# Attention scores of the second block: two heads in TensorE's row halves instead of stacked parts

## The chip, the cores and the metric

The kernel runs on one core of one Trainium2 chip. The metric is the time of one execution in device microseconds (us), the median of three runs. TensorE does the matrix products into PSUM, VectorE (DVE), ScalarE (ACT) and GpSimd (POOL) do the rest, and SyncE (SP) issues most of the DMAs.

## The reference, cut to what matters

Three transformer-like blocks follow one another on 1024 tokens. The change is in the second one, in its attention: eight query heads of 64 dimensions share two key and value heads, four query heads each, and every query looks at 1024 tokens of the sequence and 256 tokens of a context (1280 keys, no mask).

```python
def block_attention(q, k, v):
    ...
    def attend(qblk):
        s = jnp.einsum('bqkgd,bskd->bkgqs', qblk, k, preferred_element_type=jnp.float32) * scale
        p = jax.nn.softmax(s, axis=-1).astype(v.dtype)
        return jnp.einsum('bkgqs,bskd->bqkgd', p, v)
...
    q = qk_heads(p[..., OFF_Q:OFF_K], N_Q_HEADS, q_gain, rope)
    k = qk_heads(p[..., OFF_K:OFF_V], N_KV_HEADS, k_gain, rope)
...
        att = block_attention(q, jnp.concatenate([k, k_ext], axis=1), jnp.concatenate([v, v_ext], axis=1))
```

## The kernel before, in words

Products that need more precision than one pass of the type F32R gives are made of parts: a number is split into a high part and a remainder (`C.split`: a copy on ACT, a subtraction on DVE), and the products high x high, low x high and high x low are summed in PSUM. Products of F32R operands show as one weight load and one matmul each. Products of plain F32 operands show as two of each, the transposes aside.

`attention2` first makes the keys and values, and then runs a loop over 16 units; a unit is one head with one half (512) of the tokens. `scores` (from line 1219) makes for each of the unit's four tiles of 128 tokens a row of 1280 scores, in three slices of 512, 512 and 256 keys. A head has 64 dimensions, so a query tile `aQ` holds the high part in one half of the 128 partitions and the low part in the other, and the keys' tiles `aKH` and `aKL` hold the same 64 rows twice. One matmul with `aKH` (L1230) and one with `aKL` (L1231) make a slice in one PSUM bank of the tag `t`, which has two banks. The slice is then copied into the tile `P` (L1232), by ACT, or by DVE for every other short slice. `softmax_sb` (L371 to L374) takes the maximum on DVE and the exponential on ACT.

`values` calls `pv_steps` (L340 to L363): the probabilities are transposed on TensorE (L344, tag `s`), split into `pth` and `ptl` (L143, L144), and multiplied with the values (L357, tag `a`, where the product with `ptl` is 64 columns wide). At the end the sums of the softmax are spread over 64 partitions by TensorE (L1240, F32), multiplied in, and written to DRAM (L1242).

Beside the units run jobs: products of 512 tokens with a tile of the input weights (L212, L213, L215, 24 matmuls for each bank of the tag `mm`), for the gates and for the next queries. `evq` takes the queries through a norm and a rotation and splits them (L1127, L1128). The order of all instructions on each engine is written at build time by a scheduler that may move an instruction past others on its engine where data and buffers allow; on the chip each engine takes its instructions in that order, and a wait holds up all that stands behind it.

Two places elsewhere use row halves of TensorE: L2444 in the third block's scan (64 rows, 128 columns, the two halves of the partitions in two banks) and L2229 in that block's preparation (64 rows, 512 columns, one call for each half). L1295 is a product of 64 rows that uses one half alone.

Of the kernel before, what the change touches and what calls it, by code (L numbers as in the profile page):

```python
# [10 lines left out]
F32 = mybir.dt.float32  # L11
F32R = mybir.dt.float32r
# [8 lines left out]
T = 1024  # L21
D = 1024
KD = 8
HALF = (slice(0, 512), slice(512, 1024))
# [1035 lines left out]
def qk_norm(C, pool, ps, gain, rope, perm, blk2, bufs=3):  # L1060

    nc = C.nc
    n = ps.shape[1]
    new = lambda: pool.tile([128, n], F32, name="tmp", tag="tmp")
    u = pool.tile([128, n], F32, name="qu", tag="qu", bufs=bufs)
    nc.scalar.copy(u, ps)
    rb = yield from head_norm(C, pool, u, n, blk2, 1.0 / 64, 1e-6)
    nc.vector.scalar_tensor_tensor(u, u, gain, rb, op0=OP.mult, op1=OP.mult)
    if rope is None:
        return u  # L1070
    yield
    p2 = C.bank(n)
    nc.tensor.matmul(p2, perm, u, start=True, stop=True)
    q = new()
    nc.gpsimd.tensor_mul(q, u, rope[:, 0])
    t = new()
    nc.vector.tensor_mul(t, p2, rope[:, 1])
    nc.gpsimd.tensor_add(q, q, t)
    return q


def attention2(C, hx, mod, mod_rest, dr, gates):


    nc = C.nc
    NS = 1280
    with C.pool("at") as p:
        KH = p.tile([128, 2, NS], F32R, name="aKH")
        KL = p.tile([128, 2, NS], F32R, name="aKL")
        V = p.tile([128, 10, 2, 128], F32R, name="aV")  # L1090
# [27 lines left out]
        Q, new_q, nq = {}, {}, 3  # L1118

        def evq(ft, half, ps):  # L1120
            u = yield from qk_norm(C, q, ps, C.vec("q_gain"), rope[:, :, HALF[half]], perm, blk2, nq)
            for e in range(2):
                r, r2 = slice(e * 64, e * 64 + 64), slice(64 - e * 64, 128 - e * 64)
                if half == 0:
                    new_q[e] = p.tile([128, T], F32R, name="aQ", tag="aQ", bufs=3)
                t = new_q[e]
                nc.scalar.copy(t[r, HALF[half]], u[r])  # L1127
                nc.vector.tensor_sub(t[r2, HALF[half]], u[r], t[r, HALF[half]].bitcast(F32))  # L1128
                if half == 1:
                    Q[2 * ft + e] = t  # L1130

        with C.pool("atc", bufs=4) as q:
            bd = cload(C, q, "k_bd", [128, 256], "bd", 1)
# [54 lines left out]
            r = C.rsqrt(C.colsum(acc, 256, 1.0 / D, 1e-6, "s"), 2)  # L1188
# [3 lines left out]
            for k in range(KD):  # L1192
                modulated(C, q, ct[:, k, :], 256, rb, mod[:, 6, k:k + 1], mod[:, 7, k:k + 1], hc, k)
            C.add("w2_in", [4, 5], hc, KD, 256, evc)
            C.add("w2_in", [0], hx, KD, T, evq)
            C.add("w2_in", range(6, 12), hx, KD, T, evh)
            C.add("w2_in", [12, 13], hx, KD, T, evf)
            C.run()

        with C.pool("atq", bufs=4) as q:  # L1200
            nq = 2

            jobs = gates(q)
            share = sum(t for _, _, t, _ in jobs) / 512 / 16
            count, credit = [], 0.0
            for u in range(16):
                take = []
                if u in (2, 6, 10):
                    take.append((u // 4 + 1, hx, T, evq))
                credit += share  # L1210
                while jobs and credit > 0.5:
                    take.append(jobs.pop(0))
                    credit -= take[-1][2] / 512
                count.append(sum(j[2] // 512 for j in take))
                for ft, rhs, t, ev in take:
                    C.add("w2_in", [ft], rhs, KD, t, ev)
            rest = mod_rest(q)

            def scores(h, half):
                while h not in Q:  # L1220
                    C.run(1)
                    if not C.jobs:
                        C.ahead()
                kv, P, R = h // 4, [], []
                for tb in range(4):
                    t0 = half * 512 + tb * 128
                    P.append(q.tile([128, NS], F32, name="P2", tag="P2", bufs=5))
                    for s in (slice(0, 512), slice(512, 1024), slice(1024, NS)):
                        b = C.bank(s.stop - s.start, "t")
                        nc.tensor.matmul(b, Q[h][:, t0:t0 + 128], KH[:, kv, s], start=True, stop=False)  # L1230
                        nc.tensor.matmul(b, Q[h][:, t0:t0 + 128], KL[:, kv, s], start=False, stop=True)  # L1231
                        (nc.vector.tensor_copy if s.start == 1024 and tb % 2 else nc.scalar.copy)(P[tb][:, s], b)  # L1232
                    R.append(C.softmax_sb(P[tb], 0.125))
                return h, half, P, R

            def values(h, half, P, R):
                def done(o):
                    b = C.bank(512)[0:64]
                    for tb in range(4):
                        nc.tensor.matmul(b[:, tb * 128:(tb + 1) * 128], R[tb].to_broadcast([128, 64]), C.ident, start=True, stop=True)  # L1240
                    nc.vector.tensor_mul(o, o, b)
                    nc.sync.dma_start(dr["att"][(h % 2) * 64:(h % 2) * 64 + 64, h // 2, HALF[half]], o)  # L1242

                C.pv(q, P, [V[:, j, h // 4, :] for j in range(10)], None, done, "s", 2)

            prev = None
            for u in range(17):
                cur = scores(u // 2, u % 2) if u < 16 else None
                if prev:
                    values(*prev)  # L1250
                prev = cur
                C.run(count[u] if u < 16 else None)
                if u >= REST:
                    for n in range(3):
                        next(rest, None)
            C.run()
            for _ in rest:
                pass
# [670 lines left out]
class Block2:  # L1929
# [79 lines left out]
    def run(self):  # L2009
# [963 lines left out]
```

## Time and profile before

| what | value |
|---|---|
| median of 3 runs | 3925.28 us (3924.64 to 3925.58) |
| profiled execution, its time | 3927.95 us |
| profiled execution, its span | 3926.2 us |
| granted TensorE clock, mean of the span | 0.975 |
| TensorE matmuls busy | 3667.1 us (93%) |
| VectorE busy | 2926.9 us (75%) |
| ScalarE busy | 2113.3 us (54%) |

Busy time of TensorE is to be read with care: a matmul's duration in the trace covers the way of its data through the array, and the next one starts before it ends. What a matmul costs in a stream is the distance from its start to the start of the next.

### The profile page before, as it was taken

The page shows a single profiled execution, that of the slowest core. Times are in us where ns is not written, and L with a number is a line of the kernel's source. Part 1 is how long each engine was busy: PE and PEld are TensorE (multiplying, and loading weights), DVE is VectorE, ACT ScalarE, POOL GpSimd, SP SyncE. Part 2 cuts the span into 40 slices and gives each one's busy share as a digit, 9 for nine tenths or more (in the row PEclk, how much of TensorE's full clock was granted, in tenths as well). Part 3 has the DMA queues.
Part 4 walks back from the last instruction along what each step waited for, and adds up shares of the span by engine and source line. Part 5 has one row for each costly group of instructions (what it writes and reads, how often), then busy time and mean ns, then how long its engine had stood idle before and what let it go on. Part 6 is the DMA issues. An engine that isn't in the chain of part 4 may idle for free. (4 is left out here: it accounts for less than half of the span.)

```text
span 3926.2 us, 53474 instructions
## 1 busy us (share of the span) xinstructions
PE 3667.1 (93%) x19084; PEld 2864.8 (73%) x19084; DVE 2926.9 (75%) x4681; ACT 2113.3 (54%) x3248; POOL 593.9 (15%) x439
## 2 busy tenths in 40 slices
PE   7998889999999988989599999999999899989998
PEld 5786677787777667876488777777777577767776
DVE  6758867555888775666899898888988645577765
ACT  4536644436777533223578777767767543334533
POOL 2111122000000233432111000000000111320011
PEclk9999999999999999999799999999999899999999
DMA  3431125432232247656799999999999323332462
GB/s 106 137 91 46 49 94 157 155 89 86 83 101 79 73 139 242 214 192 222 254 347 381 357 353 370 353 359 369 360 348 359 113 86 123 110 108 63 120 181 71
DMA packets 303844, 739.94 MB, mean 188 GB/s; under 512 B 62711, under 2 KB 103287, under 8 KB 302168
## 3 DMA queue, kind: packets, MB, share of 16 engines
q1 hardware_dynamic: 287640, 681.72, 49.9%
q0 software_dynamic: 13632, 46.40, 4.2%
q10 hardware_dynamic: 2304, 8.39, 0.5%
q8 instruction: 150, 2.46, 0.3%
q14 instruction: 118, 0.97, 0.1%
HBM read 640.42 MB, written 89.42 MB: 186 GB/s over the span
## 5 line engine op out<-in xcount | busy, mean ns | idle before, releaser
L1772 DVE TENSOR_TENSOR ewl<-er,ewh 128x1024 fp32r<-128x1024 f32 x543 | 634.9, 1222 | 65.6 <-ACT ewh L1771 62.9
L1771 ACT CAST ewh<-er 128x1024 fp32r<-128x1024 f32 x546 | 545.5, 1051 | 63.6 <-PE s L1826 25.7
L144 DVE TENSOR_TENSOR wlo<-wlo,whi 128x1024 fp32r<-128x1024 f32 (+2 forms) x155 | 187.0, 1207 | 234.0 <-PE mm L215 143.7
L212 PE MATMUL mm<-ygh,whi 128*128 128x512 f32 x736 | 299.2, 408 | 7.2 <-ACT whi L143 3.9
L213 PE MATMUL mm<-ygl,whi 128*128 128x512 f32 x736 | 297.0, 404 | 1.2 <-DVE ygl L144 1.2
L143 ACT CAST whi<-wlo 128x1024 fp32r<-128x1024 f32 (+2 forms) x155 | 152.4, 983 | 237.3 <-PE mm L213 165.5
L215 PE MATMUL mm<-ygh,wlo 128*128 128x512 f32 x736 | 196.2, 401 | 0.0
L212 PEld LDWEIGHTS mm<-ygh,whi 128*128 128x128 f32 x736 | 140.7, 192 | 44.9 <-ACT whi L143 7.0
L1826 PE MATMUL s<-ewl,xsh 128*128 128x512 f32 x512 | 162.4, 398 | 9.9 <-DVE ewl L1772 9.9
L212 PE MATMUL mm<-hnh,whi 128*128 128x512 f32 x416 | 166.5, 400 | 1.4 <-DVE QS L306 0.9
L213 PEld LDWEIGHTS mm<-ygl,whi 128*128 128x128 f32 x736 | 140.5, 191 | 36.2 <-issue 4.2
L1826 PE MATMUL mm<-ewl,xsh 128*128 128x512 f32 x512 | 161.0, 396 | 6.3 <-DVE ewl L1772 6.3
L215 PEld LDWEIGHTS mm<-ygh,wlo 128*128 128x128 f32 x736 | 139.3, 190 | 36.1 <-issue 3.9
L1826 PE MATMUL s<-ewh,xsh 128*128 128x512 f32 x512 | 160.6, 395 | 4.9 <-ACT xsh L143 4.9
L213 PE MATMUL mm<-hnl,whi 128*128 128x512 f32 x416 | 164.7, 396 | 0.0
L1826 PE MATMUL s<-ewh,xsl 128*128 128x512 f32 x512 | 162.1, 394 | 0.0
L1826 PE MATMUL mm<-ewh,xsh 128*128 128x512 f32 x512 | 159.2, 392 | 0.5
L1826 PE MATMUL mm<-ewh,xsl 128*128 128x512 f32 x512 | 158.1, 390 | 0.0
L1772 DVE TENSOR_TENSOR ewl<-wlo,ewh 128x1024 fp32r<-128x1024 f32 x126 | 148.8, 1219 | 9.9 <-ACT ewh L1771 9.3
L1771 ACT CAST ewh<-wlo 128x1024 fp32r<-128x1024 f32 x126 | 128.9, 1054 | 16.6 <-PE s L1826 9.1
L144 DVE TENSOR_TENSOR ptl<-s,pth 128x512 fp32r<-128x512 f32 x160 | 108.0, 686 | 24.4 <-ACT pth L143 17.1
L1855 POOL DMA_INDIRECT moed<-ys,topi x16 | 57.5, 3592 | 445.5 <-DVE ys L1854 445.5
(936 smaller groups left out, 9955.2 us busy)
## 6 DMA issues: line engine op xcount, KB each, us to landing
er<-w_up SPq DMA_DIRECT2D x183, 512.0 KB, 7.0
er<-w_down SPq DMA_DIRECT2D x182, 512.0 KB, 5.7
er<-w_gate SPq DMA_DIRECT2D x181, 512.0 KB, 6.9
wlo<-w_in SPq DMA_DIRECT2D x101, 512.0 KB, 3.7
wlo<-w_up SPq DMA_DIRECT2D x45, 512.0 KB, 7.1
wlo<-w_gate SPq DMA_DIRECT2D x43, 512.0 KB, 5.9
wlo<-w_out SPq DMA_DIRECT2D x40, 512.0 KB, 3.7
wlo<-w_down SPq DMA_DIRECT2D x38, 512.0 KB, 7.2
```

Source lines behind the costliest of these rows:

```text
L143: self.nc.scalar.copy(hi, src)
L144: (eng or self.nc.vector).tensor_sub(lo, src, hi.bitcast(F32))
L212: m(b, w.hi[:, k, :], rhs.hi[:, k - k0, s], start=(k == order[0]), stop=False)
L213: m(b, w.hi[:, k, :], rhs.lo[:, k - k0, s], start=False, stop=False)
L215: m(b, w.lo[:, k, :], rhs.hi[:, k - k0, s], start=False, stop=(k == order[-1]))
L1771: nc.scalar.copy(s.hi, raw)
L1772: (nc.gpsimd if i < 6 and i % 2 == 0 else nc.vector).tensor_sub(s.lo, raw, s.hi.bitcast(F32))
L1826: m(b[n], a[:, k, :], r[:, n * 512:(n + 1) * 512], start=(k == 0 and c == 0), stop=(k == KD - 1 and c == 2))
L1855: nc.gpsimd.indirect_dma_start(out=dr["moe"], out_offset=bass.IndirectOffsetOnAxis(ap=topi[:, e:e + 1], axis=0), in_=ys, in_offset=None, c ...
```

## The change

A unit becomes a pair of heads with a quarter (256) of the tokens, 16 units as before. The query tile of a pair holds the high part of both heads, one in each half of the partitions (`aQh`), and a second tile holds the low parts (`aQl`). For each tile of 128 tokens and each slice of keys, two banks of the tag `t` are taken, one for each head, and each gets three products of 64 rows. The two heads' calls alternate in the code. The splitting of the queries becomes one copy and one subtraction over 128 partitions in place of two over 64. The tiles `P` of scores have six buffers in place of five, and the result of a unit is written in two pieces.

```diff
         def evq(ft, half, ps):
             u = yield from qk_norm(C, q, ps, C.vec("q_gain"), rope[:, :, HALF[half]], perm, blk2, nq)
-            for e in range(2):
-                r, r2 = slice(e * 64, e * 64 + 64), slice(64 - e * 64, 128 - e * 64)
-                if half == 0:
-                    new_q[e] = p.tile([128, T], F32R, name="aQ", tag="aQ", bufs=3)
-                t = new_q[e]
-                nc.scalar.copy(t[r, HALF[half]], u[r])
-                nc.vector.tensor_sub(t[r2, HALF[half]], u[r], t[r, HALF[half]].bitcast(F32))
...
+            if half == 0:
+                new_q[0] = newsp(p, [128, T], "aQ", 2)
+            t = new_q[0][:, HALF[half]]
+            C.split(t.hi, t.lo, u)
...
-                kv, P, R = h // 4, [], []
-                for tb in range(4):
-                    t0 = half * 512 + tb * 128
-                    P.append(q.tile([128, NS], F32, name="P2", tag="P2", bufs=5))
+                kv, P, R = j // 2, [None] * 4, [None] * 4
+                rows = (slice(0, 64), slice(64, 128))
+                for tb in range(2):
+                    t = slice(part * 256 + tb * 128, part * 256 + tb * 128 + 128)
+                    two = [q.tile([128, NS], F32, name="P2", tag="P2", bufs=6) for _ in rows]
                     for s in (slice(0, 512), slice(512, 1024), slice(1024, NS)):
-                        b = C.bank(s.stop - s.start, "t")
-                        nc.tensor.matmul(b, Q[h][:, t0:t0 + 128], KH[:, kv, s], start=True, stop=False)
-                        nc.tensor.matmul(b, Q[h][:, t0:t0 + 128], KL[:, kv, s], start=False, stop=True)
-                        (nc.vector.tensor_copy if s.start == 1024 and tb % 2 else nc.scalar.copy)(P[tb][:, s], b)
-                    R.append(C.softmax_sb(P[tb], 0.125))
+                        b = [C.bank(s.stop - s.start, "t") for _ in rows]
+                        for n, (x, k) in enumerate(((Q[j].hi, KH), (Q[j].lo, KH), (Q[j].hi, KL))):
+                            for e, r in enumerate(rows):
+                                nc.tensor.matmul(b[e], x[r, t], k[r, kv, s], start=(n == 0), stop=(n == 2))
+                        for e in range(2):
+                            (nc.vector.tensor_copy if s.start == 1024 and e else nc.scalar.copy)(two[e][:, s], b[e])
...
-                    nc.sync.dma_start(dr["att"][(h % 2) * 64:(h % 2) * 64 + 64, h // 2, HALF[half]], o)
+                    for e in range(2):
+                        nc.sync.dma_start(dr["att"][e * 64:e * 64 + 64, j, part * 256:part * 256 + 256], o[:, e * 256:e * 256 + 256])
```

What the scheduler makes of it on TensorE is seen at two places. The first is where the first scores stand; a number behind `t` names a bank, so 7830 and 7831 are the two heads of one slice. Before:

```order
L212 MATMUL mm_7918<-ygh,whi 128x512
L1230 MATMUL t_7833<-aKH,aQ 128x512
L1231 MATMUL t_7833<-aKL,aQ 128x512
L213 MATMUL mm_7918<-ygl,whi 128x512
L1230 MATMUL t_7837<-aKH,aQ 128x512
L1231 MATMUL t_7837<-aKL,aQ 128x512
L212 MATMUL mm_7918<-ygh,whi 128x512
```

Of the change, at the same place (all score products now have line 1231):

```order
L212 MATMUL mm_7926<-ygh,whi 128x512
L1231 MATMUL t_7830<-aKH,aQh 128x512
L1231 MATMUL t_7830<-aKH,aQl 128x512
L1231 MATMUL t_7830<-aKL,aQh 128x512
L1231 MATMUL t_7831<-aKH,aQh 128x512
L1231 MATMUL t_7831<-aKH,aQl 128x512
L1231 MATMUL t_7831<-aKL,aQh 128x512
L213 MATMUL mm_7926<-ygl,whi 128x512
```

The three products of a head moved together, and the six of a slice stand between two matmuls of a job. The second place is the start of a later unit of TensorE's order. Before:

```order
L344 MATMUL s_8268<-ident,P_7992 128x128
L1230 MATMUL t_8192<-aKH,aQ 128x512
L1231 MATMUL t_8192<-aKL,aQ 128x512
L1230 MATMUL t_8196<-aKH,aQ 128x256
L1231 MATMUL t_8196<-aKL,aQ 128x256
L344 MATMUL s_8277<-ident,P_7992 128x128
```

Of the change:

```order
L1231 MATMUL t_8210<-aKH,aQh 128x512
L1231 MATMUL t_8210<-aKH,aQl 128x512
L1231 MATMUL t_8210<-aKL,aQh 128x512
L213 MATMUL mm_8457<-ygl,whi 128x512
L212 MATMUL mm_8457<-ygh,whi 128x512
L213 MATMUL mm_8457<-ygl,whi 128x512
L212 MATMUL mm_8457<-ygh,whi 128x512
L1231 MATMUL t_8211<-aKH,aQh 128x512
L1231 MATMUL t_8211<-aKH,aQl 128x512
L1231 MATMUL t_8211<-aKL,aQh 128x512
```

Here the two heads of a slice were moved apart, with four matmuls of a job between them. Over the whole stage the 576 score products of the change stand in 120 runs (products of line 1231 with nothing else between them): 43 runs hold both heads of slices of 512 keys (one of them two slices), 21 both heads of a slice of 256 keys, 6 one head of a long slice with one of a short slice, 34 one head of a long slice alone and 16 one head of a short slice alone. TensorE's order differs in names alone up to the stage's last jobs of the queries, and again from some 700 rows behind the last score on; in between it is shifted in places.

## Rows read from the trace of the kernel before

**Rows 1.** Span and mean granted TensorE clock of the core.

```profile
core 0: 3926.2 us, clock 0.975
```

**Rows 2.** Stretches: length, busy us of PE, PEld, DVE, ACT, POOL, PEclk, DMA.

```profile
908.00:1311.00 403.00, 397.47 (x2143) 305.15 (x2143) 326.13 (x667) 307.10 (x531) 17.33 (x12) 1.00 0.27 83
1311.00:1341.00 30.00, 30.00 (x120) 21.50 (x119) 17.63 (x35) 9.43 (x13) 0.00 (x0) 1.00 0.45 142
```

**Rows 3.** Timeline, PE: start us, us, engine, line, operation, tiles, shapes, count.

```profile
909.24 0.39 PE L1230 MATMUL t<-aKH,aQ 128*128 128x512 f32 x1
909.47 0.39 PE L1231 MATMUL t<-aKL,aQ 128*128 128x512 f32 x1
...
911.09 2.03 PE L215 MATMUL mm<-ygh,wlo 128*128 128x512 f32 x8
...
913.18 0.28 PE L1230 MATMUL t<-aKH,aQ 128*128 128x256 f32 x1
913.30 0.28 PE L1231 MATMUL t<-aKL,aQ 128*128 128x256 f32 x1
```

**Rows 4.** Who waited in the attention's units: total us, times, longest.

```profile
PEld t L1230 <- ACT P L1232: 17.3, 57, 1.2
```

**Rows 5.** Line L1230 (L1231 has as many): duration ns min/median/max, first and last start, forms.

```profile
L1230 PE MATMUL t<-aKH,aQ x192: 276/396/794, 908.4 to 1294.5; 128*128 128x512 f32 x128, 128*128 128x256 f32 x64
```

**Rows 6.** Timeline, PE, around a use of both row halves in the third block.

```profile
3604.89 0.28 PE L150 MATMUL s<-uvh,ckvl 128*128 128x128 f32 x1
3605.01 0.28 PE L151 MATMUL s<-uvl,ckvh 128*128 128x128 f32 x1
3605.21 1.16 PE L2444 MATMUL mm<-TB,Z 64*128 64x128 f32 x16
3606.30 0.33 PE L149 MATMUL s<-knh,qnh 128*128 128x128 f32 x1
3606.47 0.28 PE L150 MATMUL s<-knh,qnl 128*128 128x128 f32 x1
```

**Rows 7.** Timeline, PE, around another use of both halves, 512 columns.

```profile
3166.51 2.03 PE L215 MATMUL mm<-u0h,wlo 128*128 128x512 f32 x8
3168.47 1.13 PE L2229 MATMUL s<-xwa,wa 64*128 64x512 f32 x4
3169.53 0.50 PE L212 MATMUL mm<-u1h,whi 128*128 128x512 f32 x1
3169.87 0.40 PE L213 MATMUL mm<-u1l,whi 128*128 128x512 f32 x1
```

**Rows 8.** A stream that uses one row half alone: timeline, then the line's durations.

```profile
1345.08 4.13 PE L1295 MATMUL s<-w,hc 64*128 64x512 f32 x9
...
L1295 PE MATMUL s<-w,hc x32: 589/589/694, 1345.1 to 1366.9; 64*128 64x512 f32 x32
```

**Rows 9.** Timeline, PE: narrow products of F32R in the attention's units.

```profile
930.32 1.10 PE L215 MATMUL mm<-ygh,wlo 128*128 128x512 f32 x4
931.26 0.39 PE L357 MATMUL a<-ptl,aV 128*64 128x512 f32 x1
931.49 0.60 PE L344 MATMUL s<-ident,P 128*128 128x128 f32 x4
```

**Rows 10.** Line L1232, the copies of scores, and who waited for them.

```profile
L1232 ACT COPY P<-t x160: 366/587/608, 912.2 to 1294.4; 128x512 f32<-128x512 f32 x128, 128x256 f32<-128x256 f32 x32
...
  PEld t L1230: 20.2, 67
```

**Rows 11.** Lines L1127 and L1128, the split of the queries, and who waited.

```profile
L1127 ACT CAST aQ<-tmp x16: 614/619/625, 818.6 to 1217.9; 64x512 fp32r<-64x512 f32 x16
L1128 DVE TENSOR_TENSOR aQ<-tmp,aQ x16: 684/686/1643, 820.3 to 1218.8; 64x512 fp32r<-64x512 f32 x16
...
  PE t L1230: 0.8, 1
```

**Rows 12.** Line L1242, the DMA of a unit's result.

```profile
L1242 SPq DMA_DIRECT2D dAtt<-oh x16: 451/452/469, 946.3 to 1315.0; - x16
```

More of the change, by code (lines that the diff above doesn't have):

```diff
@@ L1121, in evq @@
             u = yield from qk_norm(C, q, ps, C.vec("q_gain"), rope[:, :, HALF[half]], perm, blk2, nq)
-            for e in range(2):
-                r, r2 = slice(e * 64, e * 64 + 64), slice(64 - e * 64, 128 - e * 64)
-                if half == 0:
-                    new_q[e] = p.tile([128, T], F32R, name="aQ", tag="aQ", bufs=3)
-                t = new_q[e]
-                nc.scalar.copy(t[r, HALF[half]], u[r])
-                nc.vector.tensor_sub(t[r2, HALF[half]], u[r], t[r, HALF[half]].bitcast(F32))
-                if half == 1:
-                    Q[2 * ft + e] = t
+            if half == 0:
+                new_q[0] = newsp(p, [128, T], "aQ", 2)
+            t = new_q[0][:, HALF[half]]
+            C.split(t.hi, t.lo, u)
+            if half == 1:
+                Q[ft] = new_q[0]
         with C.pool("atc", bufs=4) as q:
@@ L1217, in attention2, with scores @@
             rest = mod_rest(q)
-            def scores(h, half):
-                while h not in Q:
+            def scores(j, part):
+                while j not in Q:
                     C.run(1)
@@ L1223, in scores, with values @@
                         C.ahead()
-                kv, P, R = h // 4, [], []
-                for tb in range(4):
-                    t0 = half * 512 + tb * 128
-                    P.append(q.tile([128, NS], F32, name="P2", tag="P2", bufs=5))
-                    for s in (slice(0, 512), slice(512, 1024), slice(1024, NS)):
-                        b = C.bank(s.stop - s.start, "t")
-                        nc.tensor.matmul(b, Q[h][:, t0:t0 + 128], KH[:, kv, s], start=True, stop=False)
-                        nc.tensor.matmul(b, Q[h][:, t0:t0 + 128], KL[:, kv, s], start=False, stop=True)
-                        (nc.vector.tensor_copy if s.start == 1024 and tb % 2 else nc.scalar.copy)(P[tb][:, s], b)
-                    R.append(C.softmax_sb(P[tb], 0.125))
-                return h, half, P, R
-            def values(h, half, P, R):
+                kv, P, R = j // 2, [None] * 4, [None] * 4
[3 more added lines that the diff above has]
+                    two = [q.tile([128, NS], F32, name="P2", tag="P2", bufs=6) for _ in rows]
+                    for s in (slice(0, 512), slice(512, 1024), slice(1024, NS)):
+                        b = [C.bank(s.stop - s.start, "t") for _ in rows]
[5 more added lines that the diff above has]
+                    for e in range(2):
+                        P[2 * e + tb] = two[e]
+                        R[2 * e + tb] = C.softmax_sb(two[e], 0.125)
+                return j, part, P, R
+            def values(j, part, P, R):
                 def done(o):
@@ L1241, in done @@
                     nc.vector.tensor_mul(o, o, b)
-                    nc.sync.dma_start(dr["att"][(h % 2) * 64:(h % 2) * 64 + 64, h // 2, HALF[half]], o)
-                C.pv(q, P, [V[:, j, h // 4, :] for j in range(10)], None, done, "s", 2)
+                    for e in range(2):
+                        nc.sync.dma_start(dr["att"][e * 64:e * 64 + 64, j, part * 256:part * 256 + 256], o[:, e * 256:e * 256 + 256])
+                C.pv(q, P, [V[:, k, j // 2, :] for k in range(10)], None, done, "s", 2)
             prev = None
             for u in range(17):
-                cur = scores(u // 2, u % 2) if u < 16 else None
+                cur = scores(u // 4, u % 4) if u < 16 else None
                 if prev:
```

## The prediction

> **What bounds the kernel now.** I read the span and clock first, then the busy times of the stretch in which the units of the attention run, then the timeline of TensorE inside it, and last the waits. The execution takes 3926.2 us from first to last instruction [rows 1], and 3927.95 us by its own time; the median of the runs shown, 3925.28 us, is 2.7 us less. I make the sum against 3927.95 and take the 2.7 off at the end. A measurement of this kernel can tell a change of about 0.2%, 8 us, from none.
>
> The units take 403 us, from 908 to 1311 us [rows 2]. TensorE shows 397 us busy in them, DVE 326 and ACT 307, and in the 30 us behind them TensorE is busy without a gap, so whatever the stage takes longer, all behind it comes later. The clock granted is 1.00 in both stretches, the level of 2.4 GHz. But 397 us of busy time is not 397 us of streaming. Eight matmuls of 512 columns take 2.03 us of which one lasts 0.39, so they start (2.03-0.39)/7 = 0.234 us apart; the two score products of 256 columns start 0.12 us apart [rows 3]. The reader should use these distances, not durations. There is also some waiting: 57 times, for 17.3 us, the first product of a score slice waits until ACT has copied the bank of an earlier one [rows 4]; with DVE's copies it is 67 times and 20.2 us [rows 10]. So TensorE is the engine that sets the pace, with roughly a twentieth of waiting in it, and the question is what the score products cost it.
>
> **Products taken out and put in.** Before there are 384 products, half of them at L1230 and half at L1231, 256 of 512 columns and 128 of 256 [rows 5]: 256 x 0.234 + 128 x 0.12 = 75.3 us. The change has 576, half of them for each half of the rows: 384 of 512 columns and 192 of 256. If the two heads always ran beside each other, they would take 192 x 0.234 + 96 x 0.12 = 56.4 us, a gain of 18.9. One after the other they take 112.9 us, a loss of 37.6.
>
> Do halves run beside each other? L2444 does just this, in F32: 16 matmuls of 128 columns in 1.16 us, one of which by its neighbours lasts 0.28, while matmuls over all rows start 0.12 us apart around it [rows 6]; 16 in a row would take 0.28 + 15 x 0.12 = 2.1 us. L2229 says the same with 512 columns: four in 1.13 us [rows 7], where nine that use one half alone take 4.13 us and last 0.59 each, so they start at most (4.13-0.59)/8 = 0.44 us apart [rows 8], and four would take 0.59 + 3 x 0.44 = 1.9 us. In both, the code's one call shows as two matmuls (16 for eight calls), so neighbours of one half come two by two and still overlap with the other half. I therefore count a run that holds both heads at the length of one, whatever its inner order. If the order did matter, a run of the form a, a, b, b, a, b would take four lengths for three and a, a, a, b, b, b five: with 29 of the first form, 21 short and 6 long of the second (from TensorE's order), some 29 x 0.23 + 21 x 0.24 + 6 x 0.47 = 15 us more. That is the upper bound; I take 0.
>
> The scheduler took a third of the pairs apart. With the runs counted in the section on the change, 44 long slices are paired, 6 runs mix a long and a short one, 34 long heads and 16 short ones stand alone: (44+6+34) x 3 x 0.234 + (21+16) x 3 x 0.12 = 59.0 + 13.3 = 72.3 us. Of the 18.9 us only 75.3 - 72.3 = **3.0 us gain** are left.
>
> **Going from all rows to halves and back.** This is the largest term, and the diff doesn't show it. Around L2444 [rows 6] the last matmul over all rows starts at 3605.01, and the second one behind the halves at 3606.47, 1.46 us later. Streamed without a stop that would be ten distances, eight pairs and one matmul over all rows at either side: ten times 0.11 to 0.12 is 1.1 to 1.2, so 0.26 to 0.36 us are lost. Around L2229 [rows 7] the last of eight L215 starts at 3166.51 + 2.03 - 0.39 = 3168.15, and L213 at 3169.87, 1.72 us later; two distances of 0.234 and two of 0.43 to 0.44 make 1.33 to 1.35, so 0.37 to 0.39 us are lost, about half on the way in (3168.15 to 3168.47 instead of 0.234, and the first pair is late by a weight load) and half on the way out (L212 to L213 0.34 instead of 0.234). The neighbours of the scores are matmuls of 512 columns as at L2229, so I take 0.38 us for a way in and out. The change has 120 of them: 120 x 0.38 = **45.6 us loss**.
>
> Against it: products of 64 columns with the F32R part `ptl` stand between full ones 150 times and more, and nothing is lost at them: L215, `ptl` and the transposes start at 931.03 (930.32 + 1.10 - 0.39), 931.26 and 931.49 [rows 9]. That is also a part of the array, and like the scores it is F32R, where L2229 and L2444 are F32. By that row the term would be 0. I go by L2229, since it has the scores' shape (64 rows, 512 columns, both halves), and keep 0 as the other end. The Trainium skill's page TensorEngine Tiling (Array Packing), section Tiling Modes, says that a change of tiling mode, as against a mere change of tile, drains TensorE. The trace agrees at L2229 and L2444 and differs at `ptl`, so the page doesn't decide between the two.
>
> **Waits.** Where a run begins at a bank that is still being copied, the stop on the way in lies beside the wait. About 0.09 us of the 0.38 is TensorE coming to rest (0.32 instead of 0.234 at L2229), so of the 67 waits that there are now, 67 x 0.09 = **6 us come back**. The other end, more waiting, is a rival below.
>
> **The rest costs nothing.** The copies of scores, the softmax, the transposes and the products with the values are as many as before. The split of the queries becomes 8 instructions on each of ACT and DVE in place of 16 of 0.62 and 0.69 us [rows 11], at most 5.0 us less on ACT and 5.5 on DVE, which have 96 and 77 us free in the stage; TensorE waited for it once, 0.8 us, and if that cover were gone this 0.8 us is its price. The results go out in 32 DMAs in place of 16; at 0.45 us each on SP's queue [rows 12] that is 16 x 0.45 = 7.2 us over 403 us, in front of loads of weights that are fetched a tile ahead (a tile feeds 48 matmuls, some 11 us); behind one DMA more, such a load still lands in time. The sixth buffer of `P` lets both heads of a first tile go ahead of the values of the unit before; while TensorE has jobs to run, that moves waiting, not work, and I take 0.
>
> **Sum.** 45.6 - 3.0 - 6 = 36.6 us: 3927.95 + 36.6 = 3964.6, less 2.7 gives 3962 us, slower by 0.9%.
>
> **Rivals.**
>
> *Switching is free for F32R* (as at `ptl`). Then only the 3.0 us are left, and what waiting goes: with the sixth buffer and slices that are made in pairs up to all 20.2 us of it could, 3922 down to 3902 us. It is faster by more than 8 us if some 5 us of waiting go along. For it speaks the F32R row, against it that both uses of row halves pay. Chance 0.16, in a little over half of it faster.
>
> *The halves don't run beside each other in F32R.* No row of F32R shows that they do. Then 37.6 us are lost in place of 3.0 gained: 3962 + 40.6 = 4003 us. Chance 0.09.
>
> *The banks become the limit.* A slice takes both banks of `t`, and the next needs both copied. ACT copies a long one in 0.59 us [rows 10], and both in 1.18. By TensorE's order, 43 of the 119 gaps between runs hold 0.46 us of work or less. Where the stops (0.38) and 0.46 cover 0.84 of the 1.18, 0.34 us is open, 43 x 0.34 = 15 us: 3977 us. Against it, ACT is busy for 307 of 403 us and in a longer stage has more room. The Trainium skill's TensorEngine Tiling (Array Packing), section Restrictions and Gotchas, says that row tiling raises the pressure on PSUM, since the row tiles write to different banks. Chance 0.12.
>
> My forecast has the remaining 0.63.
>
> **How the numbers follow.** The likeliest case has its own range from 3945 (more of the waiting goes, and the 0.26 of L2444 for each way in and out: 120 x 0.26 = 31.2) to 3977 (the inner order matters). The banks' rival lies inside or just above, with 3992 where both come together. Below, half of the first rival is taken in down to 3920. So 3920 to 3992 leaves out about 0.08 below and 0.09 above. Faster by over 0.2%: 0.09, the larger half of the first rival; within 0.2%: 0.08, the rest of it and a little of mine; slower: 0.83.
>
> **What would show it.** In the profile of the changed kernel: the two heads of a run starting a few ns apart and a pair's three products taking 0.7 us from start to start; the matmul behind a run, and the run itself, late by about 0.2 us each with no releaser named; the stage longer by some 37 us, with DVE and ACT less busy in share; the waits of line 1231 for the copies under 20 us. Wrong would be: full speed in and out of the runs (then 3902 to 3922), six products of a run 0.23 us apart each (4003), or long waits for the copies of `P`.

## The result, and the profile after

The changed kernel takes 3989.7 us (median of four runs, 3986.0 to 3997.7) where the kernel before takes 3925.0 beside it: a ratio of 1.0171, 95% interval 1.0159 to 1.0184. It is slower, as forecast, but by 65 us where 37 were worked out. The profiled execution has a span of 3989.5 us, 63.3 more than the one before [rows 1].

These stretches answer to [rows 2]. The first runs from the first score to the last, the others follow it. Columns: length, busy us of PE, PEld, DVE, ACT, POOL, then granted clock and DMA.

```profile
906.30:1339.30 433.00, 424.92 (x2216) 293.34 (x2215) 308.94 (x642) 288.71 (x505) 16.09 (x12) 1.00 0.24 74
1339.30:1379.30 40.00, 31.71 (x131) 21.11 (x128) 22.16 (x40) 12.44 (x21) 0.00 (x0) 0.83 0.29 83
1379.30:1419.30 40.00, 38.69 (x117) 21.61 (x116) 35.82 (x52) 22.43 (x31) 21.54 (x14) 0.96 0.16 53
1419.30:1459.30 40.00, 34.58 (x136) 25.17 (x135) 39.76 (x34) 11.71 (x15) 18.64 (x11) 0.96 0.28 90
```

The kernel before, cut in the same way:

```profile
908.40:1294.70 386.30, 380.77 (x2047) 292.74 (x2047) 315.86 (x647) 295.46 (x512) 17.33 (x12) 1.00 0.27 84
1294.70:1334.70 40.00, 40.00 (x191) 29.86 (x191) 23.45 (x45) 17.91 (x28) 0.00 (x0) 1.00 0.34 106
```

Two things are to be seen. The scores take 433.0 us from the first to the last where they took 386.3, with DVE and ACT busy for less of it (71% and 67%; before 82% and 76%). And directly behind the last score TensorE is now idle for 8.3 of 40 us at a mean granted clock of 0.83, where before it is busy for 40.00 of 40.00 us at 1.00.

The timeline of TensorE shows what runs of score products cost (columns as in [rows 3]):

```profile
923.65 0.39 PE L213 MATMUL mm<-ygl,whi 128*128 128x512 f32 x1
923.97 0.49 PE L1231 MATMUL t<-aKH,aQh 64*128 64x512 f32 x2
924.30 0.39 PE L1231 MATMUL t<-aKH,aQl 64*128 64x512 f32 x2
924.53 0.39 PE L1231 MATMUL t<-aKL,aQh 64*128 64x512 f32 x2
924.86 0.50 PE L212 MATMUL mm<-ygh,whi 128*128 128x512 f32 x1
925.19 0.40 PE L213 MATMUL mm<-ygl,whi 128*128 128x512 f32 x1
925.43 0.39 PE L212 MATMUL mm<-ygh,whi 128*128 128x512 f32 x1
925.75 0.50 PE L1231 MATMUL t<-aKH,aQh 64*128 64x512 f32 x1
926.09 0.39 PE L1231 MATMUL t<-aKH,aQl 64*128 64x512 f32 x1
926.09 0.50 PE L1231 MATMUL t<-aKH,aQh 64*128 64x512 f32 x1
926.32 0.39 PE L1231 MATMUL t<-aKL,aQh 64*128 64x512 f32 x1
926.43 0.39 PE L1231 MATMUL t<-aKH,aQl 64*128 64x512 f32 x1
926.66 0.39 PE L1231 MATMUL t<-aKL,aQh 64*128 64x512 f32 x1
926.98 0.50 PE L213 MATMUL mm<-ygl,whi 128*128 128x512 f32 x1
...
931.79 0.50 PE L1231 MATMUL t<-aKH,aQh 64*128 64x512 f32 x1
...
932.68 0.45 PE L357 MATMUL a<-ptl,aV 128*64 128x512 f32 x1
```

In the run at 923.97 the products of both heads start in pairs (x2), and the matmul behind it comes 0.89 us after the first of them. One head alone, from 931.79 to 932.68, takes the same 0.89: the second head is free. In the run at 925.75 the second head starts 0.34 us late (926.09), and the run takes 1.23. On the way in the first product comes 0.32 us after the job's matmul, and behind the run two matmuls follow at 0.33 each, where 0.23 is the distance in a stream.

The waits of the weight loads in the stage (who, for whom: total us, times, longest), against 17.3 us and 57 times in [rows 4]:

```profile
PEld t L1231 <- ACT P L1233: 22.6, 64, 1.1
PEld t L1231 <- issue: 12.3, 45, 0.4
PEld s L344 <- issue: 10.5, 30, 0.4
PEld a L357 <- issue: 8.7, 25, 0.4
```

The rows of "issue" (a wait with no releaser) are all but new: before, the largest in the scores, the transposes and the products with the values is 0.5 us, at L344. 95 of these 100 waits are at a run's first products or directly behind a run, where the stops are. The waits of weight loads for the copies did not shrink.

Added up over all runs of score products, from the matmul ahead to the second one behind, less the streamed distances of these two: 93.2 us in 140 runs before, 141.3 in 120 runs after. So 48.1 us of the loss lie at the runs. The whole account: 2.1 us less ahead of the stage, 46.6 more from the first score to the last, though 21 job matmuls (4.9 us) fewer stand there, 18.9 more from there until the copy of the last gate begins (241.1 us before, 260.0 after), nothing behind that: 63.4 of the 63.3.

### The profile page after: what moved, and what is told of

The parts are those of the page before. It is cut to its first block, busy times and chain, and to the rows that moved or that the text cites. A ratio compares the mean times of both kernels' runs of the same rounds, so it can differ in the third digit from the quotient of the medians.

```text
span 3989.5 us, 53821 instructions
## 1 busy us (share of the span) xinstructions
PE 3721.7 (93%) x19276; PEld 2872.6 (72%) x19276; DVE 2924.2 (73%) x4673; ACT 2101.9 (53%) x3238; POOL 592.4 (15%) x439
## 5 line engine op out<-in xcount | busy, mean ns | idle before, releaser
L212 PE MATMUL mm<-ygh,whi 128*128 128x512 f32 x736 | 304.1, 415 | 10.8 <-ACT ygh L143 4.5
```

What stands on the lines that cost most here:

```text
L212: m(b, w.hi[:, k, :], rhs.hi[:, k - k0, s], start=(k == order[0]), stop=False)
```

## The experiments

Times are medians beside the kernel before on the same chip, with 95% intervals of the ratio. One kernel's executions differ by up to half a per cent, so a trace tells more than a difference of a few us.

**The sixth buffer alone**, in the kernel before.

```diff
-                    P.append(q.tile([128, NS], F32, name="P2", tag="P2", bufs=5))
+                    P.append(q.tile([128, NS], F32, name="P2", tag="P2", bufs=6))
```

> The kernel before, with the tiles P of scores in six buffers in place of five; nothing else is changed, the score products are the stacked ones. Theory A (the changed kernel loses some 48 us at the runs of score products and some 15 us behind the last score, and the 15 come from the sixth buffer: with it TensorE's order holds no job matmul between the last score and the last product with the values, where the kernel before has 22): 3925 + 13 to 16, so 3938 to 3941 us. Theory B (the sixth buffer costs nothing, as predicted; the jobs fall behind because row halves make the scores slower): 3920 to 3927 us.

Measured: 3936.1 us, 1.0032 (1.0019 to 1.0045), 7 to 18 us slower without any row halves. The scores and the 40 us behind them:

```profile
902.80:1286.60 383.80, 376.55 (x2023) 288.60 (x2023) 311.05 (x649) 293.20 (x511) 16.78 (x12) 1.00 0.26 83
1286.60:1326.60 40.00, 33.69 (x139) 22.85 (x139) 23.65 (x44) 16.32 (x25) 0.00 (x0) 0.87 0.31 84
```

The scores take 2.5 us less than before, with 21 job matmuls (4.9 us) moved out of them, but the hole behind them is that of the changed kernel. Theory A holds here.

**The change with five buffers.**

```diff
-                    two = [q.tile([128, NS], F32, name="P2", tag="P2", bufs=6) for _ in rows]
+                    two = [q.tile([128, NS], F32, name="P2", tag="P2", bufs=5) for _ in rows]
```

> The changed kernel with five buffers of P in place of six. TensorE's order then has 35 job matmuls between the last score and the last product with the values, and 126 runs of score products in place of 120, with fewer of the form a, a, b, b, a, b and more of b, b, b, a, a, a. Theory A (the sixth buffer costs 13 to 16 us at the end of the stage): 3990 - 15 = 3975 us, with the six ways in and out and the inner order up to 6 us more, so 3974 to 3982. Theory B (the slower scores make the jobs late, whatever the buffers): 3988 to 3998 us.

Measured: 3985.0 us, 1.0155 (1.0137 to 1.0173), hardly to be told from the changed kernel and above what theory A gave. The hole is gone (40.00 of 40.00 us busy at 1.00; 247.9 us in place of 260.0 to the last gate), but the runs cost 146.6 us in place of 141.3, and the scores take 440.5 us in place of 433.0, with 25 job matmuls (5.9 us) back among them.

**All rows in place of halves**, in the changed kernel's order.

```diff
-                                nc.tensor.matmul(b[e], x[r, t], k[r, kv, s], start=(n == 0), stop=(n == 2))
+                                nc.tensor.matmul(b[e], x[:, t], k[:, kv, s], start=(n == 0), stop=(n == 2))
```

> The changed kernel, its 576 score products made over all 128 rows in place of 64 (so each head's scores are the sum of both heads'), in exactly the order of the changed kernel on every engine. No product uses row halves any more, and none lies beside another. Theory A (0.38 us for each way in and out of the halves): the products stream in 112.9 us where the runs of the changed kernel took 141.3 with their stops and waits; with some 5 to 10 us of waits left, 18 to 25 us less, 3965 to 3972 us, and the stops around the runs are gone from the trace. Rival (the late starts around the runs are weight loads or bank waits that have nothing to do with halves): they stay, and 112.9 - 72.3 = 40.6 us come on top, 4030 us.

Measured: 3978.7 us, 1.0146 (1.0122 to 1.0170), some 10 us under the change where 18 to 25 were expected: 16 us of waits are left at the runs (129.2 - 112.9). But the main claim is seen in every run. A head alone:

```profile
925.14 0.40 PE L357 MATMUL a<-pth,aV 128*128 128x512 f32 x1
925.37 0.39 PE L1231 MATMUL t<-aKH,aQh 128*128 128x512 f32 x1
925.60 0.39 PE L1231 MATMUL t<-aKH,aQl 128*128 128x512 f32 x1
925.83 0.39 PE L1231 MATMUL t<-aKL,aQh 128*128 128x512 f32 x1
926.06 0.39 PE L357 MATMUL a<-ptl,aV 128*64 128x512 f32 x1
926.29 0.40 PE L1231 MATMUL t<-aKH,aQh 128*128 128x512 f32 x1
```

All distances are 0.23. Over the 34 long heads that stand alone a run costs 0.70 us in the median here and 1.09 in the change: **a way in and out of the halves costs 0.39 us**. For the 16 short ones it is 0.40 and 0.79. The rival is out.

**The change without halves**: its units, pairs of banks, six buffers and DMAs, with stacked products; and the same with five buffers.

```diff
-                        for n, (x, k) in enumerate(((Q[j].hi, KH), (Q[j].lo, KH), (Q[j].hi, KL))):
-                            for e, r in enumerate(rows):
-                                nc.tensor.matmul(b[e], x[r, t], k[r, kv, s], start=(n == 0), stop=(n == 2))
+                        for x, k in enumerate((KH, KL)):
+                            for e in range(2):
+                                nc.tensor.matmul(b[e], Q[2 * j + e][:, t], k[:, kv, s], start=(x == 0), stop=(x == 1))
```

> The changed kernel's units (a pair of heads with a quarter of the tokens, banks taken in pairs, six buffers of P, 32 DMAs of results), but with the two stacked products of the kernel before for each slice, over all rows. It holds everything of the change but the halves. Theory A (halves cost 48 us, the sixth buffer 13 to 16, the units nothing): 3938 to 3941 us. Theory B (all of the loss is due to the halves): 3922 to 3928 us. If the units and the pairs of banks cost something of their own, it is above 3945.

> Stacked products over all rows in the change's pair units, with five buffers of P in place of six. If the loss of the stacked pair units (24 us with six buffers) is made of about 12 for the sixth buffer and about 12 for the units: 3925 + 12 = 3934 to 3942 us. If the units cost nothing of their own with five buffers: 3922 to 3930. If the buffer has no part in it: 3946 to 3950.

Measured: 3948.2 us with six, 1.0062 (1.0042 to 1.0082); 3926.3 with five, 1.0009 (0.9999 to 1.0020). So the units, the pairs of banks and the 32 DMAs cost nothing by themselves, and with the sixth buffer they lose 17 to 32 us. With six, TensorE idles for 15.0 of 397.0 us in the stage, and the hole is there; against this kernel the halves add 40.3 us at the runs (141.3 to 101.0) and 36.0 to the stage.

**Why the sixth buffer makes the hole.** In the built program the stage's tiles lie one behind the other in each partition of the on-chip memory, and the tiles `tmp` into which the gates of the next part are copied (pool `b2g`) begin at byte 156192. The stage ends at

```
before, five buffers   151968        before, six buffers   157088
change, five buffers   156064        change, six buffers   161184
```

A buffer of P takes 5120 bytes, the pairs' query tiles 4096 more than before. With six the stage reaches into `tmp`, and in ACT's order no gate of the next part is copied out before the last unit's last split of probabilities. Both banks of `mm` then hold finished jobs. In the changed kernel's trace, these two copies and who waited for them (line L1966, from 1270 us on):

```profile
L1966 ACT ACTIVATE tmp<-mm x2: 592/594/597, 1359.9 to 1360.4; 128x512 f32<-128x512 f32 x2
...
  PE mm L212: 1.3, 1
```

The last job matmul starts at 1303.7, the next one at 1360.6. Two runs keep six buffers and make room by fewer tiles elsewhere:

```diff
-        with C.pool("b2g", side="right", bufs=3) as p:
+        with C.pool("b2g", side="right", bufs=2) as p:
```

> The kernel before with six buffers of P, and two in place of three for the copied gates of the next stage, so that the stage's tiles don't reach into their place. TensorE's order has 542 job matmuls between the first and last score and 22 behind, as before. Theory A (the sixth buffer costs only by its memory): the loss of 12 us is gone, 3918 to 3928 us. Rival (six buffers are worse by themselves): 3933 to 3940 us.

(in the change `bufs=1`, and one tile `oh` in place of two)

> The changed kernel with six buffers of P, but with one buffer in place of two for a unit's result, and one in place of three for the copied gates of the next stage (the pool b2g). The stage's tiles then end below the place of those gates' copies in the on-chip memory; with two and three buffers the sixth P and the fourth query tile reach into it. TensorE's order has 27 job matmuls behind the last score again, and 561 in place of 519 between the first and the last one. Theory A (the loss behind the stage, 14 us when the moved jobs are counted, comes from the memory that the sixth buffer takes, so that jobs for the next stage can't be copied out before the last unit is done): 3973 to 3980 us, and TensorE without a gap in the 40 us behind the last score. Rival (the six buffers lose by the order of the scores themselves): 3986 to 3993 us.

Measured: the kernel before with six buffers and room 3921.3 us, 0.9988 (0.9976 to 1.0001). The loss is gone, and the hole with it, as theory A has it. (No run gives this kernel the room without the sixth buffer, so what the room alone does isn't shown.)

```profile
1289.30:1329.30 40.00, 40.00 (x193) 29.79 (x193) 23.63 (x42) 17.23 (x27) 0.00 (x0) 1.00 0.32 104
```

The change with room 3987.0 us, 1.0167 (1.0150 to 1.0184), executions from 3978.5 to 3992.8: in time not told from the change, and the expected 3973 to 3980 was missed. The trace (of the 3978.5) shows the repair at its place and a loss behind it:

```profile
1340.80:1380.80 40.00, 40.00 (x196) 30.21 (x194) 25.03 (x42) 16.11 (x25) 0.00 (x0) 1.00 0.36 114
1380.80:1420.80 40.00, 37.84 (x88) 16.75 (x86) 32.88 (x50) 17.68 (x25) 19.02 (x12) 0.78 0.16 49
1420.80:1460.80 40.00, 37.63 (x134) 26.01 (x133) 30.28 (x31) 15.60 (x19) 18.05 (x11) 0.87 0.30 99
```

Over these 120 us the changed kernel idles 15 us and loses 10 to the clock (40 x 0.17, twice 40 x 0.04); with room it idles 4.5 and loses 14 (40 x 0.22 + 40 x 0.13).

**Order or bank.** Why is the second head late in a run? My first theory was its place in the order. In the first of two runs the first product of a slice waits for both copies of the slice before, and the heads alternate; in the second it waits as well, and one head is written behind the other.

```diff
+                                if n == 0 and e == 0:
+                                    for c in free:
+                                        C.tc.add_manual_dep(m.ins, c.ins.name, mybir.DependencyInfo(mybir.DependencyClass.Sync, mybir.DependencyReason.DATA))
```

> The changed kernel, in which the first product of a slice also waits for the copies of the slice before, so that both banks are free when a run begins. TensorE's order then has 104 runs in place of 120: 51 long and 32 short ones alternate between the heads (a, b, a, b, a, b), 15 long single heads, 6 others; no run is of the form a, a, b, b, a, b any more. Theory A (0.39 us for a way in and out, and a product lies beside one of the other head only where the two stand next to each other): 104 x 0.39 + 64 us of streaming in place of 120 x 0.39 + 88, 30 us less, of which some 5 to 12 us come back as waits for the second bank: 3965 to 3972 us. Rival (the order inside a run costs nothing, as predicted): 16 x 0.39 = 6 us less, and the new waits take that back: 3984 to 3995 us.

> As the alternating kernel (the first product of a slice waits for both copies of the slice before, so both banks are free), but the three products of the first head are written ahead of the three of the second. TensorE's order then has 52 runs of the form a, a, a, b, b, b and 32 short ones of that form, 105 runs in all, where the alternating kernel has 51 and 32 of the form a, b, a, b, a, b in 104. Order theory (the second head can only begin where it stands in the order): each long run takes 1.4 us from its first product to the matmul behind it in place of 0.89, 50 x 0.4 + 30 x 0.2 = 26 us more than the alternating kernel at the runs, some 4000 us. Bank theory (the halves take their products apart from each other, and only the wait for the second head's bank makes it late): 0.9 us for each long run, and the time of the alternating kernel, 3975 to 3988 us.

Measured: alternating 3981.2 us, 1.0143 (1.0126 to 1.0160), 116.2 us at the runs; head by head 3984.5 us, 1.0159 (1.0131 to 1.0187), 120.7 us. The alternating time lies between its two forecasts; that of head by head is in the range of the bank theory. In TensorE's order a run of the latter reads

```
L1233 MATMUL t_7840<-aKH,aQh 128x512
L1233 MATMUL t_7840<-aKH,aQl 128x512
L1233 MATMUL t_7840<-aKL,aQh 128x512
L1233 MATMUL t_7841<-aKH,aQh 128x512
L1233 MATMUL t_7841<-aKH,aQl 128x512
L1233 MATMUL t_7841<-aKL,aQh 128x512
```

and in its timeline such a run is

```profile
925.45 0.51 PE L1233 MATMUL t<-aKH,aQh 64*128 64x512 f32 x2
925.79 0.41 PE L1233 MATMUL t<-aKH,aQl 64*128 64x512 f32 x2
926.03 0.41 PE L1233 MATMUL t<-aKL,aQh 64*128 64x512 f32 x2
926.36 0.50 PE L213 MATMUL mm<-ygl,whi 128*128 128x512 f32 x1
```

The products of both heads start in pairs though three of one stand ahead of three of the other; in the median of 52 long runs the second head is 0.01 us late. **The order theory fell.** It is the bank: in the run at 925.75 above, ACT's two copies end at 926.03 (L1233, 924.96 + 1.07), and the second head starts at 926.09. In 26 of the 29 runs of this form in the changed kernel it starts 0.05 us after the end of a copy. Summed over all runs of two heads, the second is 14.8 us late in the changed kernel, 1.3 us in these two.

Yet of the 25 us that the alternating kernel saves at the runs, only 10.6 are left in the stage (422.4 us): its weight loads now wait for the split probabilities. The changed kernel's rows, then the alternating kernel's:

```profile
PEld a L357 <- DVE ptl L144: 4.5, 18, 0.7
...
PEld a L357 <- ACT pth L143: 3.1, 8, 1.2
```

```profile
PEld a L357 <- DVE ptl L144: 13.4, 34, 1.0
PEld a L357 <- ACT pth L143: 10.7, 23, 1.2
```

Alternating and room together:

> Alternating heads and the room for the next stage's gates together, the two repairs of the changed kernel at once. Theory A: what is left is 106 x 0.39 = 41 us for the ways in and out, less 75 - 64 = 11 us that the overlap saves, and some 5 us more or less of waits: 25 to 35 us over the kernel before, 3950 to 3960 us. If halves could be had without loss in this way it would be 3925 or less; if neither repair works, 3985.

Measured: 3977.8 us, 1.0127 (1.0108 to 1.0146), the lowest median with halves, still 50 us behind; the 3950 to 3960 of theory A were missed. Here too the granted clock falls behind the filled hole (0.68 and 0.72 in the second and third 40 us).

**Other ways to free the second bank.** All copies of the second head on DVE; three banks for `t` and two for `s`, without and with room.

```diff
-                            (nc.vector.tensor_copy if s.start == 1024 and e else nc.scalar.copy)(two[e][:, s], b[e])
+                            (nc.vector.tensor_copy if e else nc.scalar.copy)(two[e][:, s], b[e])
...
-    BANKS = {"mm": 2, "s": 3, "t": 2, "a": 1}
+    BANKS = {"mm": 2, "s": 2, "t": 3, "a": 1}
```

> The changed kernel with all copies of the second head's scores on DVE and those of the first on ACT, so that both banks of a pair are copied at the same time. TensorE's order has 127 runs. Bank theory: the second head starts within 0.1 us of the first in most runs of two heads, the waits for the copies shrink, and the runs cost some 10 us less than 141 in spite of seven more ways in and out (2.7 us); DVE gets 64 copies of some 0.6 us, 38 us, which fit into the 124 us that it is free for in the stage: 3975 to 3985 us. If DVE's splits of the probabilities come late by them, the stage loses as much again and the time stays at 3990.

> The changed kernel with three banks for the tag t and two for s in place of two and three. TensorE's order has 82 runs in place of 120, many of them with three heads' products. If the ways in and out are what costs: 38 x 0.39 = 15 us less at the runs, and some 5 to 10 of bank waits less; against it, the transposes have one bank fewer, and may wait for the splits. 3965 to 3980 us if the transposes don't wait, about 3990 or more if they do.

> The three banks with the room for the next part's gates (one buffer for them and for a unit's result): 85 runs, 28 job matmuls behind the last score. Some 10 us below the run with three banks alone if the hole behind the last score is what it costs there: 3955 to 3970; the same time if the granted clock falls behind it as in the change with room.

Measured: copies on both 3986.0 us, 1.0165 (1.0134 to 1.0195). The second head is late by 4.5 us in all, as the bank theory has it, but 127 ways and more heads alone take the gain back (139.3 us at the runs). Three banks 4045.2 us, 1.0300 (1.0266 to 1.0333), with room 4021.0, 1.0253 (1.0224 to 1.0282). The table of banks holds for the whole program, which I had not reckoned with: 39.1 us of the loss lie behind the attention (2429.5 us from the copy of the last gate on, 2390.4 in the kernel before). It tells nothing on the banks of the scores (139.8 us at the runs). But the two with three banks differ by 24 us, 28.4 in the profiled executions. Of these, 19.2 lie in the stretch from the last score until the copy of the last gate begins (260.2 us in the one, 241.0 in the other, whose TensorE is busy all through the first 40 us):

```profile
1353.50:1393.50 40.00, 40.00 (x193) 29.27 (x191) 25.04 (x42) 16.14 (x27) 0.00 (x0) 1.00 0.33 110
1393.50:1433.50 40.00, 38.90 (x114) 18.84 (x113) 36.05 (x55) 18.99 (x27) 22.83 (x14) 1.00 0.18 59
```

So here, with halves, the room gives back what the hole took, and the clock stays up in these 80 us.

**The six products as one section**, always together, with six and with five buffers.

```diff
+                        with C.tc.tile_critical(sync_engine=mybir.EngineType.PE):
```

> The changed kernel (six buffers) with the six products of each slice written as one critical section of TensorE, which is scheduled as a whole: both heads always stand together and alternate (a, b, a, b, a, b), in 95 runs in place of 120. Each section also puts a jump in front of and behind its products, which the changed kernel doesn't have. Theory A (a way in and out costs 0.39 us, and the two heads only overlap when they alternate): 95 x 0.39 + 56 us of streaming in place of 120 x 0.39 + 88, 41 us less at the runs; some 5 to 10 us of waits for both banks come back: 3955 to 3965 us, with an alternating run of 512 columns at 1.05 us. Rival 1 (the order inside a run doesn't matter, only the ways in and out do): 25 x 0.39 = 10 us less, 3980 us. Rival 2 (the sections' jumps cost as much as they save): 3985 us and more, with stops at the jumps in the trace.

> As the run with grouped products, with five buffers of P: then 71 runs, nine of which hold several slices, and 18 job matmuls between the last score and the last product with the values. Theory A: 71 x 0.39 + 56 = 84 us at the runs plus waits, less than the 93 that the kernel before spends there with its waits, and without the sixth buffer's loss; with 10 to 13 us for the pair units 3930 to 3945 us. Rival 2 (jumps): 3960 us and more.

Measured: 4137.5 us, 1.0554 (1.0536 to 1.0573), and 4177.8, 1.0654 (1.0630 to 1.0679). Rival 2 holds: with six buffers line 1232 waited 134.9 us, 103 times, with no releaser, 1.3 us at each jump. Nothing else can be read from the time.

**Four buffers in the kernel before** (`bufs=4`).

> The kernel before with four buffers of P in place of five. TensorE's order then has 586 job matmuls between the first and the last score in place of 540, and 23 behind the last score in place of 22. If what counts is that jobs are left for the last unit, nothing is gained over five buffers, and the time is within 5 us of 3925; if jobs done inside the stage are worth more than those done behind it (the filters' part had stops and a lower granted clock), it is 3915 to 3920; if scores now wait for the buffers of P, over 3930.

Measured: 3942.0 us, 1.0057 (1.0039 to 1.0075), a loss as in the third case: the scores take 410.7 us with 46 job matmuls more (10.8 us). But no wait for a buffer of P is seen there; what grew is TensorE's wait for the split probabilities, which was 4.1 us before:

```profile
PEld a L357 <- DVE ptl L144: 12.4, 28, 2.0
```

## Why the prediction was half right

Direction and largest term stand. Two steps failed, and they make up nearly all of the difference between 37 and 63 us: the waits, and "the rest costs nothing".

*Going from all rows to halves and back*: right. 120 x 0.38 = 45.6 was taken from [rows 7]; 120 x 0.39 = 46.8 was measured by taking the halves away in the same order. The narrow F32R products [rows 9] were rightly not followed: a half of the rows costs a stop, and `ptl` none that the trace shows. Of its 160 products before, 150 are left at the full 0.23 us, and 68 of these are also entered at the full distance. The other 82 start 0.31 to 0.32 us after a `pth` product that itself follows transposes; a job matmul that stands there starts as late, so this delay isn't that of the columns. The rival of free switching is out. The Trainium skill's TensorEngine Tiling (Array Packing), section Tiling Modes, has a change of mode drain TensorE, without a price. The trace agrees for the row halves (0.39 us) and still differs at `ptl`.

*Products taken out and put in*: right. The halves run beside each other in F32R (0.89 us for one head and for two, where both banks are free), whatever the order inside the run, as I had counted them; the rival that they don't is out.

*Waits*: the step that failed at the runs. "67 x 0.09 = 6 us come back" went by the wait at a run's first bank. But a slice now wants two banks, and the second is copied 0.5 us after the first. At the runs, before 93.2 - 75.3 = 17.9 us were waits; after it is 141.3 - 46.8 - 72.3 = 22.2. So **4 us more in place of 6 less**. By place (17.6 and 21.9 us in this count, with rounded distances): ahead of a run's first product they fell from 9.2 us to 4.3, so most of the 6 us did come back; inside and behind the runs they rose from 8.4 to 17.6, and 14.8 of these are the second head's lateness. (The 22.6 us of the row above are other waits, 59 of its 64 at a run's first weight load, under matmuls that still run; that the sums agree is chance.) The wait for the second bank is the mechanism of my rival of the banks, which I kept apart from the sum with a chance of 0.12. That it comes to the rival's 15 us is in part luck: the rival had 0.34 us in 43 gaps, while 29 long runs are late by 0.36 us in the median and other runs give the rest. The Trainium skill's TensorEngine Tiling (Array Packing), section Restrictions and Gotchas, has row tiling raise the pressure on PSUM; the trace agrees, with these 14.8 us. Pair units without halves show the same sum of waits at 25.7 us (101.0 - 75.3) with six buffers and some 15 with five, and the halves with five buffers 21, so what of the 4 us is due to the halves and what to the sixth buffer no run separates. With them, 46.8 - 3.0 + 4.3 = 48.1 us. The stage is 46.6 us longer, with 4.9 us of jobs moved out of it and some 3 of other waits added.

*The rest costs nothing*: wrong in one place. Of the sixth buffer I wrote that it "moves waiting, not work". It also takes memory, that of the next part's gate copies, and TensorE has no jobs behind the last score: 18.9 us later on, 4.9 of them the 21 jobs that moved there, so **14 us where I took 0**. The cause is shown in the kernel before (lost with six, back with room); in the stacked pair units six lose and five don't. With halves it shows in time between the two runs of three banks (4045.2 and 4021.0). In the changed kernel itself the traces show the hole go, with five buffers and with room (the profiled span is 13.6 us shorter, 3975.9), but the times hardly show the gain: the medians fall by 4.7 and 2.7 us, less than executions differ. The copies, the softmax, the queries' split and the DMAs do cost nothing: stacked pair units with five buffers, 1.0009.

What stays open: in four of the five versions with pair units in which the hole is gone, the granted clock falls to 0.68 to 0.78 in the next 40 us and takes part of the gain; in the fifth (three banks with room) and in the kernel before it is 1.00 there. One of the four, the stacked pair units with five buffers, uses no halves in its scores, and its profiled execution has the lowest mean clock (0.971, the others 0.972 to 0.978) of those that make its 1.0009; so how often the clock falls isn't known from one profile each. In the change with room it falls after 14 half-row products of the filters in a row, which had waited 1.21 us. The kernel before has ten there, then one full matmul and four more (the nine of [rows 8] are cut by that view's window). What in this makes it fall no run separates.

## What to carry to other kernels

Count how often a kernel enters and leaves row halves and price each by a neighbour of the same shape. Here a paired long slice saves 0.23 us (three distances of 0.234 for both heads in place of four), and a way in and out costs 0.39; so by this estimate even a perfect pairing loses with one slice for each run, and a run needs two or more to pay, which no kernel here settles. A second product beside the first is free only if its bank is free too; that wait lies inside a run, where TensorE is busy with the other head, and shows as no idle time of its matmuls. And before a pool gets one buffer more, look at what lies behind it in memory and in the program.

## What the runs showed of the hardware that was not expected

The two halves go each at its own pace: six products that stand as a, a, a, b, b, b in TensorE's order start in pairs, 0.01 us apart in the median. So the fourth starts ahead of the second and third: that an engine takes its instructions in order, as said of the kernel before, holds for each half here and not across the two. And where the hole was filled in the change with room, the half clock came some 60 us later; in the kernel before with room it did not (1.00 over the 80 us behind the last score). TensorE's timeline of the change with room, in the filters:

```profile
1393.30 6.27 PE L1299 MATMUL s<-w,hc 64*128 64x512 f32 x14 [1.21 <-ACT hc L944]
...
1401.43 1.12 PE L1299 MATMUL s<-w,hc 64*128 64x512 f32 x2 [0.72 <-DVE hfb L1300]
...
1405.93 2.07 PE L1299 MATMUL s<-w,hc 64*128 64x512 f32 x2
1407.94 0.79 PE L213 MATMUL mm<-ygl,whi 128*128 128x512 f32 x1
```

From 1403 on two of them take 2.07 us in place of 1.12, and a full matmul 0.79 in place of 0.40: 1.2 in place of 2.4 GHz.
